# A decoder layer whose weights are split into two fp32r halves: three engines put into program order while Strassen products run

## The chip, the cores and the metric

One core of one Trainium2 chip. The metric is the device time of one execution in microseconds (us). TensorE is called PE here (PEld is its weight load), VectorE DVE, ScalarE ACT, GpSimd POOL and SyncE SP; SP issues the loads.

## The reference

One layer of a hybrid decoder, batch 1, 256 rows, D = 2048, all in fp32:

```
x <- LN0(alpha*x + 0.5*SwiGLU_1(x))                      # FFN 1, 2048 -> 2 x 5504 -> 2048
z  = x @ W_in                                            # nine column groups
m  = sigmoid(gate_conv)*(yA @ Wa) + sigmoid(gate_hgrn)*(yB @ Wb)   # short conv | gated recurrence
x <- LN1(alpha*x + m @ W_out)
x <- LN2(alpha*x + 0.5*SwiGLU_2(x))                      # FFN 2
x <- LN3(alpha*x + sigmoid(x @ W_pg) * (p @ W_pp))
swiglu(x, w_in, w_out): a, u = split(x @ w_in); return (silu(a) * u) @ w_out
```

## The kernel before

**Matrix products.** Every fp32 operand is held as a sum of two fp32r halves, high (h) and low (l), and a product is three matmuls: wh by xh, wl by xh, wh by xl (`passes`, L1052 to L1054). The 256 rows are two row tiles (t = 0, 1) of 128; a pass works on two k blocks of 128 rows of a weight and 512 columns.

**The way of a weight.** SP loads a piece of 256 x 512 into a tile `raw` (`weight_dma`, four of them); ACT casts it to its high half wh (`weight_cast`, L986); DVE subtracts that from raw and gets wl (`weight_split`, L997). There are six pairs of wh and wl (NMAIN) and a few more outside the FFNs (EXTRA). When PE has used a pair up, `consumed` calls `feed`, which issues whatever load, add, cast and split has room.

**An FFN** has 11 chunks of at most 512 columns of a and u. Chunks 0 and 1 are plain products. Chunks 2 to 10 are `Quad`s: one level of Strassen, seven products p1 to p7 in place of eight, with weight sums on DVE (`weight_add`, L965) in tiles of the rings 11, 12, 21, 22. The part of k that doesn't fill a whole step is done by a short step (`ORDER`, 59 passes in a Quad) or by plain passes (`ORDER8`, 60 passes); chunk 2 has the second, chunks 3 to 10 the first. What follows a Quad's products is five steps, `first` to `fifth` in `in_units`: copies on ACT, adds of banks on DVE (`both`, L471), a silu, a product. `turn` then makes the result an operand of the second matrix, three ticks later (a tick is a pass): four transposes on PE into the one bank for transposes (L275), a cast to gh on ACT (L285), a subtraction to gl on DVE (L286). After each of the chunks 2 to 9 come two `out_unit`s, products with w_out of the chunks before; each adds its result to x on DVE (L534).

**Layer norms.** The normalised x is made an operand at once (transposes on PE, `yT` on ACT, L424, xh, xl); g and b are applied to x itself later, in `affine_rows`, one of four column chunks at a time. Before FFN 2 their rows come into one tile, `region["spare"]`, one after the other; `sums`, which makes the Strassen sums of x, waits for that (`settle`).

**What sets the order.** Work is emitted in the program's order with deferred steps (`defer`, by ticks). A tile scheduler then sets each engine's order of instructions by its own timeline; what stands on an engine runs strictly in that order, each instruction waiting for what it needs. FFN 1 runs from 0 to about 700 us of the span, the mixer to 1405, the stage `lead2` and FFN 2 to 2110, then the embedding's product.

Of the kernel before, what the change touches and what calls it, by code (L numbers as in the profile page):

```python
# [10 lines left out]
F32 = mybir.dt.float32  # L11
# [3 lines left out]
ALU = mybir.AluOpType  # L15
PSUM = bass.MemoryType.PSUM

P = 128
D = 2048
S = 256  # L20
NT = 2
DFF = 5504
CW = 1024
CC = 512
# [112 lines left out]
def hybrid_layer(ctx: ExitStack, tc: tile.TileContext, x, p, ln_g, ln_b, ffn1_w_in, ffn1_w_out, mix_w_in,  # L137
                 conv_w, hg_lower_bound, hg_norm_w, branch_w_conv, branch_w_hgrn, mix_w_out,
                 ffn2_w_in, ffn2_w_out, ple_w_gate, ple_w_proj, out):
    nc = tc.nc  # L140
# [7 lines left out]
    op = pool("op", side="left")  # L148
# [4 lines left out]
    region = {}  # L153
# [8 lines left out]
    def open_region(kind):  # L162


        if kind.startswith("tail"):
            region.pop("hctx").close()
        region["pool"] = reopen("ctx", kind, "left")
        region["kind"] = kind
        if kind.startswith("lead"):
            region["high"] = reopen("hctx", kind + "h", "right")  # L170
            held.update(dict.fromkeys(HIGH, 0), on=False)
            region["spare"] = high("11", "spare")
        if kind.startswith("ffn"):
            roles = {"a": 7, "t": 1}
        else:
            roles = {"t": 2, "a": 4, "h": 2}
        free = deque(sorted(banks, key=lambda n: used_at[n]))
        for role, n in roles.items():
            role_of[role] = [free.popleft() for _ in range(n)]
# [5 lines left out]
    ps = pool("ps", space=PSUM)  # L185
# [16 lines left out]
    def defer(delay, fn):  # L202
        insort(later, (state["tick"] + delay, fn), key=lambda e: e[0])
# [37 lines left out]
    def settle(c):  # L241

        while c in unsettled:
            later.pop(0)[1]()
# [63 lines left out]
    def high(part, name):  # L308

        return region["high"].tile([P, KG, CC], F32, tag="b" + part, name=name, bufs=HIGH[part])  # L310
# [5 lines left out]
        return plain[t, c // 2][:, c % 2, :]  # L316

    def sums(stat):
        for c in range(4):
            settle(c)  # L320

        def both(o, a, b, op):
            nc.vector.tensor_tensor(out=o, in0=a, in1=b, op=op)

        def four(x11, x12, x21, x22, s1, s2, s3, s4):
            both(s3, x11, x21, ALU.subtract)
            both(s1, x21, x22, ALU.subtract)
            both(s2, s1, x11, ALU.subtract)
            both(s4, x12, s2, ALU.add)

        lo, hi, spare = [plain[t, 0] for t in range(NT)], [plain[t, 1] for t in range(NT)], region["spare"]
        x = [lo[0][:, 0, :], lo[0][:, 1, :], lo[1][:, 0, :], lo[1][:, 1, :]]
        s3 = spare[:, 0, :]

        def low_sums():
            four(*x, x[2], x[0], s3, x[1])

        def made(n, src):
            halves(stat, n, 0, src, 4, "s")


        short = spare[:, 1, :]

        def short_sums():
            y = [hi[t][:, 0, i * P : (i + 1) * P] for t in range(NT) for i in range(2)]
            four(*y, *(short[:, i * P : (i + 1) * P] for i in range(4)))

        def made_short():
            halves(stat, "short", 0, short, 4, "s")
            h, l = stat.parts["short", 0]  # L350
            for i in range(4):
                stat.parts[f"s{i + 1}", 1] = h[:, i : i + 1, :], l[:, i : i + 1, :]

        def delta(c):
            d = hi[0][:, c % 2, :]
            both(d, d, hi[1][:, c % 2, :], ALU.subtract)
            halves(stat, "d", c, d, 4, "s")

        todo = (low_sums, lambda: made("s1", x[2]), lambda: made("s2", x[0]), lambda: made("s3", s3),
                lambda: made("s4", x[1]), short_sums, made_short, lambda: delta(2), lambda: delta(3),  # L360
                lambda: held.update(on=True))
        for i, fn in enumerate(todo):
            defer(1 + 2 * i, fn)
# [30 lines left out]
        nc.vector.bn_aggr(mv, stats[t])  # L394
        return mv[:, 0:1], rsqrt_of(mv[:, 1:2], 1, 1.0, LN_EPS / scale ** 2)

    def affine_rows(i, c, ts, gb, delay):

        if gb is None:
            gb = rp.tile([P, KG, CC], F32, tag="raw", name="gb", bufs=NRAW)  # L400
        for a, src in enumerate((ln_g, ln_b)):
            nc.sync.dma_start(gb[:, a, :], src[0, i : i + 1, c * CC : (c + 1) * CC].broadcast_to([P, CC]))

        def apply():
            for t in ts:
                xc = xt[t][:, c * CC : (c + 1) * CC]
                nc.vector.tensor_tensor(out=xc, in0=xc, in1=gb[:, 0, :], op=ALU.mult)
                nc.vector.tensor_tensor(out=xc, in0=xc, in1=gb[:, 1, :], op=ALU.add)
            unsettled.remove(c)

        defer(delay, apply)

    def layer_norm(t, i, scale, stat):

        mean, r = moments(t, scale)

        def operand(c, xc):
            y = plain_tile(t, c) if stat is x2 else st.tile([P, CC], F32, tag="silu", name="y", bufs=2)
            tp = transposed(xc, 4)
            if t == 0 and c < 2:  # L420
                gate["pe"] = state["turned"], 1
            for a in range(4):
                k = i * 16 + 4 * c + a
                nc.scalar.activation(y[:, a * P : (a + 1) * P], tp[:, a * P : (a + 1) * P], AF.Identity,  # L424
                                     bias=gbT[:, 48 + k : 49 + k], scale=gbT[:, k : k + 1])
            halves(stat, t, c, y, 4, "x")

        for c in range(4):
            xc = xt[t][:, c * CC : (c + 1) * CC]
            norm = nc.vector.tensor_scalar(out=xc, in0=xc, scalar1=mean, scalar2=r, op0=ALU.subtract, op1=ALU.mult)  # L430
            defer((4 if t else 7 if stat is x2 else 6) + c, lambda c=c, xc=xc: operand(c, xc))
            if c == 1 and t == 0:
                gate["lo"] = norm.ins, 2
        if t == NT - 1:
            for c in range(4):
                unsettled.add(c)
                if stat is x2:
                    defer(2 + 8 * c, lambda c=c: affine_rows(i, c, range(NT), region["spare"], 6))
                else:
                    defer(40 + 20 * c, lambda c=c: affine_rows(i, c, range(NT), None, 4))  # L440

    def layer_norm_out(t, gb):
        mean, r = moments(t, 1.0)
# [9 lines left out]
    def ffn(name, xs, w_in, w_out, ln_i, nxt):  # L453
# [7 lines left out]
        def in_units(ch, g, ci):  # L461
            c0 = starts[ch]
            w = starts[ch + 1] - c0
            if ch > 1:
                made = {}

                def work(tag):
                    return st.tile([P, CC], F32, tag=tag, name=tag, bufs=2 if tag == "silu" else 3)

                def both(o, a, b, op):  # L470
                    nc.vector.tensor_tensor(out=o, in0=a, in1=b, op=op)  # L471

                def first(ps):
                    made["c11"] = work("h")
                    nc.scalar.copy(made["c11"], ps["p1"])

                def second(ps):
                    c = made["c12"] = work("silu")
                    nc.scalar.copy(c, ps["p3"])
                    both(c, c, ps["p5"], ALU.add)  # L480

                def third(ps):
                    e = made["e"] = work("silu")
                    made["c22"] = work("h")
                    both(e, made["c11"], ps["p6"], ALU.add)
                    both(made["c12"], made["c12"], e, ALU.subtract)
                    both(e, e, ps["p7"], ALU.add)
                    both(made["c22"], ps["p5"], e, ALU.subtract)

                def fourth(ps):  # L490
                    h = made["c11"]
                    both(h, h, ps["p2"], ALU.add)
                    nc.scalar.activation(h, h, AF.Silu)
                    both(h, h, made["c12"], ALU.mult)
                    turn(g, 0, ci, h, CC)

                def fifth(ps):
                    e = made["e"]
                    both(e, e, ps["p4"], ALU.add)
                    nc.scalar.activation(e, e, AF.Silu)  # L500
                    both(e, e, made["c22"], ALU.mult)
                    turn(g, 1, ci, e, CC)

                after = deque([(("p1",), first), (("p3", "p5"), second), (("p6", "p7"), third),
                               (("p2",), fourth), (("p4",), fifth)])
                units.append(Quad(xs, w_in, (c0, DFF + c0), CC, after, ch > 2))
                return
            silu = {}

# [564 lines left out]
    def run_quad(u, gi):  # L1074
# [17 lines left out]
            gi += 1  # L1092
        return gi

    gi = 0
    for u in units:
        if isinstance(u, Unit):
            gi = run_unit(u, gi)
        elif isinstance(u, Quad):
            gi = run_quad(u, gi)  # L1100
        else:
            if u[0] == "merge":
                u[1]()
            if region["kind"] != u[0]:
                open_region(u[0])
            if u[0] != "merge":
                u[1]()
            feed()
# [30 lines left out]
```

## Time and profile before

| | |
|---|---|
| median of three runs | 2227.24 us (2227.22 to 2227.46) |
| the profiled execution | 2226.91 us, its span 2225.1 us |
| mean granted PE clock | 0.995 of full speed |
| PE busy | 2192.7 us, 10062 instructions |
| DVE busy | 1753.5 us |
| ACT busy | 1155.2 us |
| DMA | 430 MB, 193 GB/s |

An engine's busy time is how long it worked within the span; the idle time of an engine matters only where another waits for it. In rows of the trace the first number is the start in us, the second how long one instruction or a run of xN takes, then engine, line, operation and tiles (out<-in), and in brackets the idle time just before it and what ended that. The granted clock is the share of full speed that the throttle gave PE.

### The profile page before, as it was taken

The page shows a single profiled execution, that of the slowest core. Times are in us where ns is not written, and L with a number is a line of the kernel's source. Part 1 is how long each engine was busy: PE and PEld are TensorE (multiplying, and loading weights), DVE is VectorE, ACT ScalarE, POOL GpSimd, SP SyncE. Part 2 cuts the span into 40 slices and gives each one's busy share as a digit, 9 for nine tenths or more (in the row PEclk, how much of TensorE's full clock was granted, in tenths as well). Part 3 has the DMA queues.
Part 4 walks back from the last instruction along what each step waited for, and adds up shares of the span by engine and source line. Part 5 has one row for each costly group of instructions (what it writes and reads, how often), then busy time and mean ns, then how long its engine had stood idle before and what let it go on. Part 6 is the DMA issues. An engine that isn't in the chain of part 4 may idle for free.

```text
span 2225.1 us, 27081 instructions
## 1 busy us (share of the span) xinstructions
PE 2192.7 (99%) x10062; PEld 1828.1 (82%) x10062; DVE 1753.5 (79%) x2042; ACT 1155.2 (52%) x1357; POOL 9.8 (0%) x32
## 2 busy tenths in 40 slices
PE   9999999999999999999999999899999999999997
PEld 7987888888887888888888888798788888888886
DVE  6788999999985678567555875669899999999667
ACT  5555565555555434444444443655556555556463
POOL 1000000000000000000000000000000000000000
PEclk9999999999999999999999999999999999999999
DMA  7656666666663665544565655576566666665564
GB/s 252 224 185 198 208 205 190 190 207 208 199 196 118 201 195 171 185 157 151 189 195 183 205 194 192 167 241 188 185 198 204 204 212 194 202 204 188 173 221 152
DMA packets 225848, 430.00 MB, mean 193 GB/s; under 512 B 14252, under 2 KB 22964, under 8 KB 225716
## 3 DMA queue, kind: packets, MB, share of 16 engines
q1 hardware_dynamic: 225716, 428.27, 60.4%
q8 instruction: 79, 1.29, 0.2%
q14 instruction: 53, 0.43, 0.1%
HBM read 426.12 MB, written 2.10 MB: 192 GB/s over the span
## 4 chain that ended last, share of the span: by engine, by line
PE 91%; DVE 5%; DMA 2%; issue 1%; ACT 1%; SPq 0%; DVEq 0%; ACTq 0%
PE bank L1053 29%; PE bank L1054 29%; PE bank L1052 29%; DVE wl L997 2%; PE bank L275 2%; PE bank L644 1%; DVE raw L965 1%; DMA raw<-in_ffn_w_in_dram 1%; DMA spare<-in_ln_g_dram 1%; ACT wh L986 1%; DMA raw<-in_ffn_w_out_dram 0%; DVE x L446 0%; DVE x L447 0%; ACT y L424 0%; DVE x L430 0%
## 5 line engine op out<-in xcount | busy, mean ns | idle before, releaser
L986 ACT CAST wh<-raw 128x1024 fp32r<-128x1024 f32 (+2 forms) x944 | 959.8, 1032 | 833.8 <-PE bank L1054 519.1
L997 DVE TENSOR_TENSOR wl<-raw,wh 128x1024 fp32r<-128x1024 f32 (+2 forms) x944 | 1113.4, 1200 | 286.8 <-ACT wh L986 266.1
L1054 PE MATMUL bank<-wh,xl 128*128 128x512 f32 (+1 forms) x1688 | 652.7, 387 | 5.0 <-DVE xl L286 4.9
L1053 PE MATMUL bank<-wl,xh 128*128 128x512 f32 (+1 forms) x1688 | 652.9, 388 | 0.5 <-DVE wl L997 0.3
L1052 PE MATMUL bank<-wh,xh 128*128 128x512 f32 (+1 forms) x1688 | 648.3, 388 | 1.8 <-ACT xh L285 1.8
L1054 PEld LDWEIGHTS bank<-wh,xl 128*128 128x128 f32 x1688 | 317.9, 188 | 66.5 <-DVE xl L286 6.3
L1052 PEld LDWEIGHTS bank<-wh,xh 128*128 128x128 f32 x1688 | 318.0, 188 | 62.1 <-ACT xh L285 2.5
L1053 PEld LDWEIGHTS bank<-wl,xh 128*128 128x128 f32 x1688 | 318.1, 188 | 61.5 <-DVE wl L997 1.6
L1053 PE MATMUL bank<-wl,gh 128*128 128x512 f32 x896 | 350.6, 392 | 4.5 <-DVE wl L997 4.3
L1054 PE MATMUL bank<-wh,gl 128*128 128x512 f32 x896 | 350.2, 392 | 0.0
L1052 PE MATMUL bank<-wh,gh 128*128 128x512 f32 x896 | 348.9, 393 | 0.0
L965 DVE TENSOR_TENSOR raw<-raw,raw 128x1024 f32<-128x1024 f32 (+1 forms) x176 | 206.3, 1172 | 6.4 <-DMA raw<-in_ffn_w_in_dram 4.7
L1053 PEld LDWEIGHTS bank<-wl,gh 128*128 128x128 f32 x896 | 168.7, 188 | 40.8 <-DVE wl L997 6.4
L1054 PEld LDWEIGHTS bank<-wh,gl 128*128 128x128 f32 x896 | 168.8, 188 | 34.7
L1052 PEld LDWEIGHTS bank<-wh,gh 128*128 128x128 f32 x896 | 168.6, 188 | 34.3 <-ACT gh L285 0.2
L1053 PE MATMUL bank<-wl,sh 128*128 128x512 f32 x464 | 180.8, 390 | 0.0
L1054 PE MATMUL bank<-wh,sl 128*128 128x512 f32 x464 | 180.8, 390 | 0.0
L1052 PE MATMUL bank<-wh,sh 128*128 128x512 f32 x464 | 179.4, 390 | 0.0
L1054 PEld LDWEIGHTS bank<-wh,sl 128*128 128x128 f32 x464 | 87.2, 188 | 18.1
L1053 PEld LDWEIGHTS bank<-wl,sh 128*128 128x128 f32 x464 | 87.2, 188 | 18.0
L1052 PEld LDWEIGHTS bank<-wh,sh 128*128 128x128 f32 x464 | 87.2, 188 | 18.0
L534 DVE TENSOR_TENSOR x<-x,bank 128x512 f32<-128x512 f32 x64 | 43.6, 682 | 21.6 <-PE bank L1054 21.6
(175 smaller groups left out, 1003.6 us busy)
## 6 DMA issues: line engine op xcount, KB each, us to landing
raw<-in_ffn_w_in_dram SPq DMA_DIRECT2D x288, 512.0 KB, 4.4
raw<-in_mix_w_in_dram SPq DMA_DIRECT2D x176, 512.0 KB, 4.7
raw<-in_ffn_w_out_dram SPq DMA_DIRECT2D x168, 512.0 KB, 4.6
raw<-in_ffn_w_in_dram SPq DMA_DIRECT2D x64, 256.0 KB, 3.1
raw<-in_mix_w_out_dram SPq DMA_DIRECT2D x32, 512.0 KB, 5.3
raw<-in_ple_w_gate_dram SPq DMA_DIRECT2D x32, 512.0 KB, 5.1
raw<-in_ffn_w_in_dram SPq DMA_DIRECT2D x32, 384.0 KB, 4.0
raw<-in_branch_w_conv_dram SPq DMA_DIRECT2D x16, 512.0 KB, 5.4
```

Of the source, the lines that this page charges most:

```text
L275: state["turned"] = nc.tensor.transpose(tp[:, i * P : (i + 1) * P], src[:, i * P : (i + 1) * P], ident).ins
L534: nc.vector.tensor_tensor(out=xc, in0=xc, in1=acc, op=ALU.add)
L644: nc.tensor.matmul(gp[:, (h * 2 + t) * 64 : (h * 2 + t + 1) * 64], kd[:, h, t * P : (t + 1) * P], qd[:, h, t, :], start=True, stop=True)
L965: nc.vector.tensor_tensor(out=out, in0=a, in1=b, op=ALU.add)
L986: nc.scalar.copy(h[:, :n, :w], raw[:, :n, :w])
L997: nc.vector.tensor_tensor(out=l[:, :n, :w], in0=raw[:, :n, :w], in1=h[:, :n, :w].bitcast(F32), op=ALU.subtract)
L1052: nc.tensor.matmul(acc, sh, wh[:, a, :n], start=first, stop=False)
L1053: nc.tensor.matmul(acc, sh, wl[:, a, :n], start=False, stop=False)
L1054: nc.tensor.matmul(acc, sl, wh[:, a, :n], start=False, stop=last)
```

## The change

1. From the first Quad of an FFN until the next stage, ACT, DVE and SP run their instructions in program order (`manual_schedule`); the scheduler still sets PE's order.
2. The rows of g and b for the x of FFN 2 are loaded into operand tiles of the tags gh and gl, early (2, 5, 8, 11 ticks after the norm), and applied 12, 14, 16, 18 ticks later. `sums` doesn't wait for them any more, and takes its spare tile from ring 11.
3. Chunk 2 uses the short step too. Three adds and products that follow a Quad are put off by one tick.

```diff
@@ sums
-        for c in range(4):
-            settle(c)
-        lo, hi, spare = [plain[t, 0] for t in range(NT)], [plain[t, 1] for t in range(NT)], region["spare"]
+        lo, hi, spare = [plain[t, 0] for t in range(NT)], [plain[t, 1] for t in range(NT)], high("11", "s")
@@ affine_rows
-        if gb is None:
+        if early:
+            rows = [op.tile([P, CC], F32, tag=tag, name="gb", bufs=8) for tag in ("gh", "gl")]
+        else:
             gb = rp.tile([P, KG, CC], F32, tag="raw", name="gb", bufs=NRAW)
...
-        defer(delay, apply)
+        defer(12 + 2 * c if early else 4, apply)
@@ layer_norm
-                if stat is x2:
-                    defer(2 + 8 * c, lambda c=c: affine_rows(i, c, range(NT), region["spare"], 6))
-                else:
-                    defer(40 + 20 * c, lambda c=c: affine_rows(i, c, range(NT), None, 4))
+                early = stat is x2
+                defer(2 + 3 * c if early else 40 + 20 * c, lambda c=c, early=early: affine_rows(i, c, early))
@@ in_units: second, fourth, fifth
-                    both(c, c, ps["p5"], ALU.add)
+                    defer(1, lambda: both(c, c, ps["p5"], ALU.add))
...
-                    both(h, h, made["c12"], ALU.mult)
+                    defer(1, lambda: both(h, h, made["c12"], ALU.mult))
...
-                    both(e, e, made["c22"], ALU.mult)
+                    defer(1, lambda: both(e, e, made["c22"], ALU.mult))
...
-                units.append(Quad(xs, w_in, (c0, DFF + c0), CC, after, ch > 2))
+                units.append(Quad(xs, w_in, (c0, DFF + c0), CC, after, True))
@@ the loop over units
+    ordered = ExitStack()
+    in_order = {mybir.EngineType.DVE, mybir.EngineType.Activation, mybir.EngineType.SP}
...
         elif isinstance(u, Quad):
+            if "ordered" not in region:
+                region["ordered"] = ordered.enter_context(tc.manual_schedule(engines=in_order))
             gi = run_quad(u, gi)
...
+            if u[0].startswith("tail"):
+                ordered.close()
+                region.pop("ordered")
```

The program has 9891 rows on PE in place of 9897 (six matmuls fewer), 2053 on DVE in place of 2043, 1347 on ACT in place of 1342, 896 on SP in place of 892. Lines of the changed kernel stand 1 to 5 lower (L983 is the cast of L986, L994 the split of L997, L962 the weight sum of L965, L284 and L285 the operand's cast and subtraction, L274 the transposes, L468 the adds of banks, L531 the update of x). Names below carry buffer numbers, which differ between the two kernels.

**FFN 1, the end of chunk 4, ACT.** The product of the chunk is `h` and `silu`; gh are its two operand tiles, wh the weights' high halves. Before:

```order
L986 CAST wh_2301<-raw_2204 128x1024
L986 CAST wh_2313<-raw_2216 128x1024
L986 CAST wh_2325<-raw11_2039 128x1024
L986 CAST wh_2337<-raw_2234 128x1024
L285 CAST gh_2264<-bank1_80 128x512
L500 ACTIVATE silu_2218<-silu_2218 128x512
L986 CAST wh_2378<-raw12_2329 128x1024
L986 CAST wh_2390<-raw21_2146 128x1024
L986 CAST wh_2401<-raw_2249 128x1024
L285 CAST gh_2278<-bank1_80 128x512
L986 CAST wh_2413<-raw21_2146 128x512
```

Three weight casts stood between the two gh casts and four ahead of the first. Now, the same place:

```order
L983 CAST wh_2258<-raw_2199 128x1024
L497 ACTIVATE silu_2231<-silu_2231 128x512
L284 CAST gh_2277<-bank1_80 128x512
L284 CAST gh_2291<-bank1_80 128x512
L983 CAST wh_2314<-raw_2217 128x1024
L983 CAST wh_2326<-raw_2229 128x1024
L983 CAST wh_2338<-raw11_2052 128x1024
L983 CAST wh_2350<-raw_2247 128x1024
```

The two gh casts stand together, and the four weight casts that stood ahead of them stand behind.

**The same place, PE.** `bank1` holds the transposes, and bank6 and bank7 are an out unit's. Before, around the second four transposes (the cast behind gh_2278, wh_2413, is used 42 matmuls further on):

```order
L1052 MATMUL bank7_86<-wh_2313,gh_1790 128x512
L1053 MATMUL bank7_86<-wl_2314,gh_1790 128x512
L1054 MATMUL bank7_86<-wh_2313,gl_1791 128x512
L275 MATMUL bank1_80<-ident_87,silu_2218 128x128 x4
L1052 MATMUL bank3_82<-wh_2325,xh_303 128x512
L1053 MATMUL bank3_82<-wl_2326,xh_303 128x512
L1054 MATMUL bank3_82<-wh_2325,xl_304 128x512
```

The transposes stood behind the out unit, at the next Quad's beginning. Now:

```order
L1050 MATMUL bank7_86<-wl_2259,gh_1315 128x512
L1051 MATMUL bank7_86<-wh_2258,gl_1316 128x512
L274 MATMUL bank1_80<-ident_87,silu_2231 128x128 x4
L1049 MATMUL bank6_85<-wh_2314,gh_1789 128x512
L1049 MATMUL bank7_86<-wh_2314,gh_1803 128x512
L1050 MATMUL bank6_85<-wl_2315,gh_1789 128x512
L1051 MATMUL bank6_85<-wh_2314,gl_1790 128x512
```

They stand inside the out unit, and the matmul right behind them uses wh_2314, the cast right behind the second gh cast on ACT.

**The same place, DVE, now.** gl are the low halves of the chunk's operand tiles:

```order
L468 TENSOR_TENSOR silu_2231<-silu_2231,h_2232 128x512
L285 TENSOR_TENSOR gl_2278<-bank1_80,gh_2277 128x512
L285 TENSOR_TENSOR gl_2292<-bank1_80,gh_2291 128x512
L531 TENSOR_TENSOR x0_94<-x0_94,bank0_79 128x512
L994 TENSOR_TENSOR wl_2315<-raw_2217,wh_2314 128x1024
L994 TENSOR_TENSOR wl_2327<-raw_2229,wh_2326 128x1024
```

The split wl_2315 stands behind both gl and the update of x; the splits of these weights stood ahead of both gl before.

**FFN 1, the end of chunk 2, DVE.** `silu<-h,bank` is an add of `third` that waits for a bank of the Quad. Before:

```order
L997 TENSOR_TENSOR wl_1225<-raw_1087,wh_1224 128x1024
L471 TENSOR_TENSOR silu_1242<-h_1151,bank4_83 128x512
L997 TENSOR_TENSOR wl_1237<-raw_1139,wh_1236 128x512
L997 TENSOR_TENSOR wl_1255<-raw_1195,wh_1254 128x1024
L471 TENSOR_TENSOR silu_1197<-silu_1197,silu_1242 128x512
```

The last weights of the Quad were split behind that add. Now:

```order
L994 TENSOR_TENSOR wl_1220<-raw_1035,wh_1219 128x1024
L994 TENSOR_TENSOR wl_1238<-raw_1100,wh_1237 128x1024
L994 TENSOR_TENSOR wl_1250<-raw_1152,wh_1249 128x512
L468 TENSOR_TENSOR silu_1255<-h_1164,bank7_86 128x512
L468 TENSOR_TENSOR silu_1210<-silu_1210,silu_1255 128x512
```

Three splits stand ahead of it.

**Between mixer and FFN 2, ACT, now.** yT and xh are the operand tiles of the normalised x, the table load and silu belong to chunk 0:

```order
L423 ACTIVATE yT_11207<-bank2_81,gbT_96 128x128 x4
L423 ACTIVATE yT_11207<-bank6_85,gbT_96 128x128 x4
L509 ACT_TABLE_LOAD
L509 ACTIVATE silu_11375<-bank7_86 128x512
L284 CAST xh_11216<-yT_11207 128x512
L423 ACTIVATE yT_11248<-bank2_81,gbT_96 128x128 x4
```

The table load and the silu stood behind all xh casts of both row tiles before.

More of the change, by code (lines that the diff above doesn't have):

```diff
@@ L171, in open_region @@
             held.update(dict.fromkeys(HIGH, 0), on=False)
-            region["spare"] = high("11", "spare")
         if kind.startswith("ffn"):
@@ L395, in moments, with affine_rows @@
         return mv[:, 0:1], rsqrt_of(mv[:, 1:2], 1, 1.0, LN_EPS / scale ** 2)
-    def affine_rows(i, c, ts, gb, delay):
-        if gb is None:
+    def affine_rows(i, c, early):
+        if early:
+            rows = [op.tile([P, CC], F32, tag=tag, name="gb", bufs=8) for tag in ("gh", "gl")]
+        else:
             gb = rp.tile([P, KG, CC], F32, tag="raw", name="gb", bufs=NRAW)
-        for a, src in enumerate((ln_g, ln_b)):
-            nc.sync.dma_start(gb[:, a, :], src[0, i : i + 1, c * CC : (c + 1) * CC].broadcast_to([P, CC]))
+            rows = [gb[:, a, :] for a in range(2)]
+        for w, src in zip(rows, (ln_g, ln_b)):
+            nc.sync.dma_start(w, src[0, i : i + 1, c * CC : (c + 1) * CC].broadcast_to([P, CC]))
         def apply():
-            for t in ts:
+            for t in range(NT):
                 xc = xt[t][:, c * CC : (c + 1) * CC]
-                nc.vector.tensor_tensor(out=xc, in0=xc, in1=gb[:, 0, :], op=ALU.mult)
-                nc.vector.tensor_tensor(out=xc, in0=xc, in1=gb[:, 1, :], op=ALU.add)
+                nc.vector.tensor_tensor(out=xc, in0=xc, in1=rows[0], op=ALU.mult)
+                nc.vector.tensor_tensor(out=xc, in0=xc, in1=rows[1], op=ALU.add)
             unsettled.remove(c)
-        defer(delay, apply)
+        defer(12 + 2 * c if early else 4, apply)
     def layer_norm(t, i, scale, stat):
```

## The prediction

> **What bounds the kernel now.** I read the page first: part 1, part 4, then the steady stretch as windows, and last the places where TensorE stands, engine by engine in time.
>
> ```profile
> PE 2192.7 (99%) x10062; PEld 1828.1 (82%) x10062; DVE 1753.5 (79%) x2042; ACT 1155.2 (52%) x1357; POOL 9.8 (0%) x32
> ...
> PE 91%; DVE 5%; DMA 2%; issue 1%; ACT 1%; SPq 0%; DVEq 0%; ACTq 0%
> ...
> raw<-in_ffn_w_in_dram SPq DMA_DIRECT2D x288, 512.0 KB, 4.4
> ```
>
> PE is busy 99% of 2225.1 us and is 91% of the chain that ended last. So the only ways to a better time are fewer matmuls and shorter PE stalls, and every new PE stall is paid in full. One chunk of each FFN (the same instruction of chunks next to each other) shows it closer; columns are the stretch in us, its length, busy time and count of PE, weight load, DVE, ACT, POOL, then the granted clock, DMA share and GB/s:
>
> ```profile
> 311.65:374.51 62.86, 62.86 (x282) 52.06 (x282) 57.77 (x59) 35.88 (x38) 0.00 (x0) 1.00 0.65 201
> 1718.76:1781.62 62.86, 62.86 (x282) 52.06 (x282) 57.76 (x59) 35.88 (x38) 0.00 (x0) 1.00 0.64 201
> ```
>
> PE has no idle time at all; DVE, with 57.8 of 62.9 us, is the next bound, and ACT and DMA are far off. So the casts and splits keep up now, but DVE can catch up on no more than 5 us per chunk.
>
> Stalls stand elsewhere. At the end of chunk 2, the first Quad of an FFN (rows of DVE, then of PE, in time; in brackets the idle time before the row and what ended it):
>
> ```profile
> 189.58 0.69 DVE L471 TENSOR_TENSOR silu<-h,bank 128x512 f32<-128x512 f32 x1 [2.61 <-PE bank L1054]
> 190.18 1.22 DVE L997 TENSOR_TENSOR wl<-raw,wh 128x1024 fp32r<-128x1024 f32 x1
> ...
> 192.50 0.40 PE L1054 MATMUL bank<-wh,xl 128*128 128x512 f32 x1
> 194.93 0.50 PE L1053 MATMUL bank<-wl,gh 128*128 128x512 f32 x1 [2.02 <-DVE wl L997]
> ...
> 1599.66 0.39 PE L1052 MATMUL bank<-wh,gh 128*128 128x512 f32 x1
> 1600.15 0.50 PE L1053 MATMUL bank<-wl,xh 128*128 128x512 f32 x1
> ...
> 1601.18 0.40 PE L1054 MATMUL bank<-wh,xl 128*128 128x512 f32 x1
> 1603.62 0.50 PE L1053 MATMUL bank<-wl,gh 128*128 128x512 f32 x1 [2.05 <-DVE wl L997]
> ```
>
> DVE waited 2.61 us for a bank with splits queued behind that row, and PE paid: start to start 2.43 us where a matmul takes 0.23. The granted clock after it:
>
> ```profile
> 192.20:195.60 3.40, 1.38 (x6) 0.80 (x6) 3.40 (x4) 0.63 (x1) 0.00 (x0) 1.00 0.54 154
> 195.70:199.00 3.30, 3.30 (x9) 2.56 (x8) 3.30 (x6) 0.36 (x1) 0.00 (x0) 0.50 0.73 236
> 199.10:202.50 3.40, 3.40 (x16) 2.79 (x16) 2.18 (x3) 1.28 (x2) 0.00 (x0) 1.00 0.91 301
> 1601.90:1605.30 3.40, 1.68 (x7) 1.40 (x8) 3.40 (x5) 0.06 (x1) 0.00 (x0) 1.00 0.48 167
> 1605.40:1608.80 3.40, 3.40 (x17) 2.80 (x16) 3.40 (x6) 1.05 (x1) 0.00 (x0) 1.00 0.91 308
> ```
>
> After 3.4 us with PE busy 1.38 (idle 2.02) the clock was 0.50 for the next 3.4 us; after 3.4 us with 1.68 busy (idle 1.72) it stayed 1.00. A slow stretch fits 8 or 9 matmuls where a full one fits 15 (3.41 / 0.227): it costs 7 x 0.227 = 1.6 us.
>
> **The change, part by part.**
>
> *Matmuls.* Chunk 2 with the short step has 59 passes instead of 60; a pass fewer is three matmuls, twice: 6 x 0.227 = -1.4 us. The pitch is from this pair, 27 starts apart, (402.72 - 396.58) / 27 = 0.2274:
>
> ```profile
> 396.58 0.40 PE L1052 MATMUL bank<-wh,gh 128*128 128x512 f32 x1
> ...
> 402.72 0.39 PE L1052 MATMUL bank<-wh,gh 128*128 128x512 f32 x1
> ```
>
> *The end of chunk 2.* In the new order of DVE three splits stand ahead of the add that waits for the bank, so PE's next weights are ready when that wait comes. Lost there now: 2.43 - 0.23 = 2.2 in each FFN, 1.6 for the slow stretch in the first, and some 0.95 in each for three or four starts that come 0.1 to 0.3 us late (1599.66 to 1600.15 is one, 0.49 where 0.23 would do): 4.4 + 1.6 + 1.9 = 7.9. I take all of it as gone: -7.9 (bounds 0 and -7.9).
>
> *The ends of chunks 2 to 9: a new wait.* This is the costly part. In the new program order of ACT both gh casts of a chunk's product stand next to each other and the next weight cast behind them; the second gh cast waits for the second four transposes, and the matmul that stands right behind those transposes on PE needs that weight cast. On DVE both gl and an x update stand ahead of its split. Before, 42 matmuls (9.6 us) lay between the transposes and the first use of the cast behind the second gh. The order shows the pattern 8 times in each FFN, 16 in all. Durations for the chain, all from one place of the steady stretch:
>
> ```profile
> 394.75 0.60 PE L275 MATMUL bank<-ident,h 128*128 128x128 f32 x4
> 395.11 0.48 PE L1052 MATMUL bank<-wh,gh 128*128 128x512 f32 x1
> 395.42 0.40 PE L1053 MATMUL bank<-wl,gh 128*128 128x512 f32 x1
> 395.66 0.40 PE L1054 MATMUL bank<-wh,gl 128*128 128x512 f32 x1
> ...
> 395.39 0.59 ACT L285 CAST gh<-bank 128x512 fp32r<-128x512 f32 x1 [0.71 <-PE bank L275]
> 395.87 0.64 ACT L500 ACTIVATE silu<-silu 128x512 f32<-128x512 f32 x1
> ...
> 403.82 0.59 ACT L285 CAST gh<-bank 128x512 fp32r<-128x512 f32 x1 [2.52 <-PE bank L275]
> ...
> 406.86 1.05 ACT L986 CAST wh<-raw 128x1024 fp32r<-128x1024 f32 x1 [0.75 <-PE bank L1054]
> ...
> 395.52 0.68 DVE L534 TENSOR_TENSOR x<-x,bank 128x512 f32<-128x512 f32 x1
> 396.11 1.22 DVE L997 TENSOR_TENSOR wl<-raw,wh 128x1024 fp32r<-128x1024 f32 x1
> 397.25 0.69 DVE L286 TENSOR_TENSOR gl<-bank,gh 128x512 fp32r<-128x512 f32 x1
> 397.85 0.68 DVE L471 TENSOR_TENSOR silu<-silu,h 128x512 f32<-128x512 f32 x1
> ...
> 404.44 0.69 DVE L286 TENSOR_TENSOR gl<-bank,gh 128x512 fp32r<-128x512 f32 x1 [0.56 <-ACT gh L285]
> ```
>
> Counting from the end of the transposes (395.35): gh starts at +0.04, the next ACT instruction 0.48 later (395.39 to 395.87), and the weight cast takes 1.05: PE can go on at about +1.6. DVE: gl starts 0.62 after gh (403.82 to 404.44), its pitch is 0.60 (397.25 to 397.85), the x update's 0.59 (395.52 to 396.11), the split takes 1.22: +0.04 +0.62 +0.60 +0.59 +1.22 = 3.07, and PE's first matmul with that split at about +3.1. Unstalled it starts as the third behind the transposes, at +0.31 (395.66). So a place costs 3.1 - 0.3 = 2.8 us. The lower bound is 2.3 (without the x update), the upper 3.4 (DVE one 0.6 us row late); each step is forced by the order of one engine, so I see no cover. 16 x 2.8 = +45.
>
> *The clock at these places.* The stall leaves PE idle for 2.6 us in two pieces (0 to 1.55 and 2.05 to 3.1). A 3.41 us window catches 2.02 of it, which halved the clock above, in 43% of phases, and 1.72, which did not, in 60%: 7 to 10 of the 16 places. I take 8 x 1.6 = +13; bounds 0 and 16 x 1.6 = 26.
>
> The Trainium skill, "TensorE: Matmul & The Clock Gate", section "What's actually happening", gives the slow clock to the default state and to one at least wholly idle window of some 3.4 us. No place here would empty a window, so by it the +13 is 0 and the sum 2265. The trace disagrees: the window at 192.20 was busy 1.38 us and the next ran at 0.50.
>
> *Rows of g and b in operand tiles.* Between the mixer and the second FFN:
>
> ```profile
> 1415.07 0.69 DVE L407 TENSOR_TENSOR x<-x,spare 128x512 f32<-128x512 f32 x1 [2.84 <-DMA spare<-in_ln_g_dram]
> ...
> 1417.67 0.80 PE L1054 MATMUL bank<-wh,xl 128*128 128x512 f32 x1 [4.20 <-DVE xl L286]
> ...
> 1439.09 1.28 ACT L512 ACT_TABLE_LOAD   x1
> 1440.38 0.60 ACT L512 ACTIVATE silu<-bank 128x512 f32<-128x512 f32 x1
> ```
>
> DVE waits 2.84 us for a row of g, and PE stands 4.20 us for xl behind it. With the rows loaded early that wait goes; but the xh cast ahead of this xl stands behind a weight cast that waits for its own load, and six multiplies of 0.60 (3.6 us) come into DVE's queue: I cost this at 0. The table load and silu (1.28 + 0.60), last on ACT now, stand in the new order ahead of xh casts of the second row tile: +2, what they take. Bounds -5 (4.20 and a slow stretch gone in part) and +5. Take +2.
>
> *The rest.* DVE gets ten rows more, ACT five, SP four. At 1.2 us DVE's are 12 us, hidden under PE with 2225 - 1754 = 471 us idle; without that cover 12. The load queue SP now issues strictly in program order, a load behind one whose slot is late: with 4.4 us to landing and DMA at 0.65 I cost it at 0; a load that is late adds up to 4.4. The multiplies put off by a tick move nothing on PE: 0, or 0.6 each on a chunk where DVE is late.
>
> **Sum**, on the profiled execution's span: 2225.1 - 1.4 - 7.9 + 45 + 13 + 2 = 2275.8. That execution took 2226.91 us, 1.8 beyond its span, and the median of the three runs is 0.3 above it: 2278.
>
> **Rivals.**
>
> 1. The clock stays at 1.00 at the 16 places: 2278 - 13 = 2265. For it, 1603.62 (idle 1.72 in its window, no slow stretch); against it, 195.70.
> 2. It halves at nearly all: 2278 + 13 = 2291. The stalls recur at one spacing, so the phases need not be spread.
> 3. DVE becomes the bound inside the Quads: in program order each of its waits for a bank holds back the splits, as the 2.61 us did. At 0.5 us in each of 18 Quads +9, 2287; at the 2.02 us of 194.93 +36, 2314. Against it: 5 us of slack per chunk, and the added stalls give DVE time.
> 4. The other side, not slower: the queued casts at the 16 places are covered after all, because ACT and DVE reach them while PE still has matmuls whose weights are split. It decides at (7.9 + 1.4) / 16 = 0.58 us a place: below that the kernel is faster; with nothing lost, 2227.2 - 9.3 = 2218. For it speaks only that DVE and ACT kept pace in the steady chunk; against it, that the weight cast stands behind the gh cast and that behind the transposes, with no matmul between them and the one that needs it.
> 5. The change does not do what it says: excluded, the new rows stand in program order.
>
> **How the numbers follow.** Chances: main case (7 to 10 slow windows, 2270 to 2286) 0.50; rival 1, 0.18; rival 2, 0.11; rival 3, 0.14; rival 4, 0.06; something else 0.01. The predicted time is the main case's, 2278. The range: from below 16 x 2.3 and no slow stretch, 2227.2 - 9.3 + 37 - 2 = 2253; from above 16 x 3.4 with 16 slow stretches, 2227.2 - 9.3 + 54 + 26 + 2 = 2300. What this measurement can tell from no change is about 0.2%, 4.5 us. Only rival 4 and a remainder end below 2231.7: slower 0.94, faster 0.05, same 0.01.
>
> **What would show it.** In the changed kernel's waits, PE should wait 16 times for the weight cast and 16 times for its split, each pair behind four transposes, 2.8 us together; the chunk period should go from 62.9 to 65.7 or 67.3; the granted clock should fall to 0.50 behind about half of these places; the 2 us waits at 194.93 and 1603.62 should be gone; PE's busy share should drop to some 97%. I am wrong if PE has matmuls left while the second gh cast runs, if the split is there at +1.6, or if DVE's waits for banks grow.

## The result and the profile after: 3.6% slower, more than the range allowed

The changed kernel took 2309.38 us in the median of four runs (2306.75 to 2310.1), the kernel before 2227.35 beside it: a ratio of 1.0363 with a 95% interval of 1.035 to 1.0376. The direction was right, the size was not: +82 us in place of +51, and 9 us above the range's upper end. The profiled execution took 2309.94 us with a span of 2308.2, 83.1 more than before.

From the page of the changed kernel, the busy time of the engines and the chain that ended last:

```profile
PE 2228.3 (97%) x10056; PEld 1838.1 (80%) x10056; DVE 1768.8 (77%) x2052; ACT 1141.8 (49%) x1362; POOL 10.1 (0%) x32
...
PE 81%; DVE 9%; ACT 5%; issue 3%; DMA 2%; ACTq 0%; DVEq 0%; SPq 0%
```

PE is 81% of the chain in place of 91%, ACT and DVE have 14% in place of 6%. PE's busy time rose by 36 us with six matmuls fewer, so none of it is work: 13 more windows of 3.41 us at the slow clock (20 in place of 7), at 1.6 us each, are 21 of them; the other 15 were not assigned. What PE waited for, in us in total, times, and the longest:

```profile
PE bank L1049 <- ACT wh L983: 33.1, 31, 1.6
PE bank L1050 <- DVE wl L994: 16.6, 18, 2.8
```

The kernel before has no such line for the cast. Two chunks, from one second set of transposes to the next, in the columns used for the windows before:

```profile
414.15:481.62 67.47, 65.08 (x283) 53.09 (x282) 58.09 (x58) 34.52 (x38) 0.00 (x0) 0.97 0.58 187
481.62:548.38 66.76, 63.96 (x282) 51.84 (x281) 58.00 (x58) 34.52 (x38) 0.00 (x0) 1.00 0.59 189
```

A chunk takes 67.5 us with a slow stretch in it and 66.8 without, where it took 62.9. One of the 16 places in time, PE, ACT, DVE:

```profile
481.62 0.60 PE L274 MATMUL bank<-ident,silu 128*128 128x128 f32 x4
483.83 0.73 PE L1049 MATMUL bank<-wh,gh 128*128 128x512 f32 x2 [1.62 <-ACT wh L983]
485.34 0.50 PE L1050 MATMUL bank<-wl,gh 128*128 128x512 f32 x1 [0.78 <-DVE wl L994]
...
482.25 0.58 ACT L284 CAST gh<-bank 128x512 fp32r<-128x512 f32 x1 [2.63 <-PE bank L274]
482.73 3.89 ACT L983 CAST wh<-raw 128x1024 fp32r<-128x1024 f32 x4
...
482.87 0.69 DVE L285 TENSOR_TENSOR gl<-bank,gh 128x512 fp32r<-128x512 f32 x1 [2.52 <-ACT gh L284]
483.48 0.68 DVE L531 TENSOR_TENSOR x<-x,bank 128x512 f32<-128x512 f32 x1
484.07 3.49 DVE L994 TENSOR_TENSOR wl<-raw,wh 128x1024 fp32r<-128x1024 f32 x3
```

The chain is the forecast one: transposes end at 482.22, PE goes on 1.61 us later with wh and 3.12 us later with wl. All 16 places look so; each costs 2.9 us in late starts. A second kind of stall, which the prediction's sum does not have, stands inside Quads:

```profile
526.85 1.22 DVE L962 TENSOR_TENSOR raw<-raw,raw 128x1024 f32<-128x1024 f32 x1
529.26 2.36 DVE L994 TENSOR_TENSOR wl<-raw,wh 128x1024 fp32r<-128x1024 f32 x2 [1.19 <-ACT wh L983]
...
528.18 2.00 ACT L983 CAST wh<-raw 128x1024 fp32r<-128x1024 f32 x2 [2.50 <-DVE raw L962]
...
530.23 0.50 PE L1049 MATMUL bank<-wh,gh 128*128 128x512 f32 x1 [0.40 <-ACT wh L983]
```

DVE makes a weight sum, ACT waits for it and casts it, and DVE waits 1.19 us for the cast: the split is next in its order, and nothing behind it can pass. PE catches up with the casts and waits 0.40 us. At the end of FFN 1, behind another such sum, PE waited 2.65 us for a split:

```profile
670.46 0.50 PE L1050 MATMUL bank<-wl,gh 128*128 128x512 f32 x1 [2.65 <-DVE wl L994]
```

Adding up PE's late starts (start to start beyond 0.227 us for a matmul) in both traces gives where the 83 us are (the stalls of the kernel before that the prediction puts at the end of chunk 2 are at the end of chunk 3, see below):

| | us |
|---|---|
| the 16 places, 2.93 each | +46.9 |
| slow clock behind 10 of them, 1.6 each | +16 |
| 11 stalls of 0.66 to 0.78 inside Quads | +8.1 |
| ends of FFN 1 and FFN 2, slow stretches included | +13.4 |
| between mixer and FFN 2 (13.9 in place of 9.8) | +4.1 |
| start of the mixer (5.1 in place of 3.0) | +2.1 |
| end of chunk 3, both FFNs | -7.8 |
| six matmuls | -1.4 |
| not assigned | +1.7 |

### The profile page after: what moved, and what is told of

Its sections match the earlier page's. It is cut to its first block, busy times and chain, and to the rows that moved or that the text cites. A ratio compares the mean times of both kernels' runs of the same rounds, so it can differ in the third digit from the quotient of the medians.

```text
span 2308.2 us, 27063 instructions
## 1 busy us (share of the span) xinstructions
PE 2228.3 (97%) x10056; PEld 1838.1 (80%) x10056; DVE 1768.8 (77%) x2052; ACT 1141.8 (49%) x1362; POOL 10.1 (0%) x32
## 4 chain that ended last, share of the span: by engine, by line
PE 81%; DVE 9%; ACT 5%; issue 3%; DMA 2%; ACTq 0%; DVEq 0%; SPq 0%
PE bank L1050 26%; PE bank L1051 26%; PE bank L1049 26%; DVE wl L994 4%; ACT wh L983 3%; DVE raw L962 3%; PE bank L274 1%; DMA raw<-in_ffn_w_out_dram 1%; PE bank L641 1%; ACT gh L284 0%; ACT y L423 0%; DVE x L443 0%; DVE x L531 0%; DVE x L444 0%; DMA raw<-in_ffn_w_in_dram 0%
## 5 line engine op out<-in xcount | busy, mean ns | idle before, releaser
L983 ACT CAST wh<-raw 128x1024 fp32r<-128x1024 f32 (+2 forms) x948 | 948.1, 1030 | 868.9 <-PE bank L1051 385.2
L994 DVE TENSOR_TENSOR wl<-raw,wh 128x1024 fp32r<-128x1024 f32 (+2 forms) x948 | 1117.4, 1197 | 281.2 <-ACT wh L983 261.8
L1049 PE MATMUL bank<-wh,xh 128*128 128x512 f32 (+1 forms) x1682 | 639.4, 389 | 6.2 <-ACT xh L284 3.0
L1050 PE MATMUL bank<-wl,gh 128*128 128x512 f32 x896 | 358.9, 401 | 14.8 <-DVE wl L994 14.8
L1050 PEld LDWEIGHTS bank<-wl,xh 128*128 128x128 f32 x1682 | 317.3, 189 | 63.2 <-DVE wl L994 2.1
L1051 PE MATMUL bank<-wh,gl 128*128 128x512 f32 x896 | 357.0, 399 | 0.0
L962 DVE TENSOR_TENSOR raw<-raw,raw 128x1024 f32<-128x1024 f32 (+1 forms) x180 | 209.9, 1166 | 2.8 <-DMA raw<-in_ffn_w_in_dram 1.6
L1049 PE MATMUL bank<-wh,sh 128*128 128x512 f32 x468 | 172.8, 392 | 0.1
L285 DVE TENSOR_TENSOR gl<-bank,gh 128x512 fp32r<-128x512 f32 (+2 forms) x50 | 33.2, 666 | 64.3 <-ACT gh L284 64.3
```

The source lines that it names most:

```text
L285: nc.vector.tensor_tensor(out=lf, in0=src, in1=hf.bitcast(F32), op=ALU.subtract)
L962: nc.vector.tensor_tensor(out=out, in0=a, in1=b, op=ALU.add)
L983: nc.scalar.copy(h[:, :n, :w], raw[:, :n, :w])
L994: nc.vector.tensor_tensor(out=l[:, :n, :w], in0=raw[:, :n, :w], in1=h[:, :n, :w].bitcast(F32), op=ALU.subtract)
L1049: nc.tensor.matmul(acc, sh, wh[:, a, :n], start=first, stop=False)
L1050: nc.tensor.matmul(acc, sh, wl[:, a, :n], start=False, stop=False)
```

## The experiments

Theory A was that the casts queued behind the gh casts make the loss; theory B, that DVE's program order does; theory C, that the other parts have a share. Two more came after the first four runs: theory D, that in program order DVE is the bound, and theory E, that what is left are fixed waits of PE at a few instructions.

**Without the program order.**

```diff
-            if "ordered" not in region:
-                region["ordered"] = ordered.enter_context(tc.manual_schedule(engines=in_order))
...
-            if u[0].startswith("tail"):
-                ordered.close()
-                region.pop("ordered")
```

> The changed kernel without the program order: ACT, DVE and SP are set by the scheduler as before; the rows of g and b in operand tiles and the short step in chunk 2 stay. Theory A (the loss is the program order): 2218 to 2230 us, no wait for a weight cast behind transposes. Theory C (the other two parts carry a share of the loss, by the rows' loads or the new step): 2240 us or more.

2232.93 us, ratio 1.0023 (1.0011 to 1.0035): between the two forecasts, 3 us above A's and 7 below C's. So the program order carries nearly all of the loss. The rest of the change costs 5 us by itself. Without the order the stalls at the ends of the first Quads are not gone, and there are three in place of two: chunk 2, with the short step now, stalls in both FFNs (4.2 us around 134, 4.3 at 1543), chunk 3 in FFN 2 alone (4.3 at 1608). DVE at the end of chunk 2 in this run:

```profile
128.73 0.69 DVE L468 TENSOR_TENSOR silu<-h,bank 128x512 f32<-128x512 f32 x1 [2.77 <-PE bank L1051]
```

**The program order and nothing else.**

```diff
+    ordered = ExitStack()
+    in_order = {mybir.EngineType.DVE, mybir.EngineType.Activation, mybir.EngineType.SP}
...
         elif isinstance(u, Quad):
+            if "ordered" not in region:
+                region["ordered"] = ordered.enter_context(tc.manual_schedule(engines=in_order))
             gi = run_quad(u, gi)
...
+            if u[0].startswith("tail"):
+                ordered.close()
+                region.pop("ordered")
```

> The kernel before with the program order on ACT, DVE and SP and nothing else of the change (chunk 2 as before, rows of g and b through the spare tile). If the order is the loss and the other two parts matter little under it: 2300 to 2320 us. If the other two parts save time once the order is fixed (the 7.9 us at chunk 2): above 2315 us, and the wait at the end of chunk 2 stays.

2305.55 us, 1.035 (1.032 to 1.0381). The waits at the end of chunk 3 are gone here too, and nothing else of the change is in this run: so the -7.8 us come from the order. The short step of chunk 2 has no part in them.

**One engine at a time.**

```diff
-    in_order = {mybir.EngineType.DVE, mybir.EngineType.Activation, mybir.EngineType.SP}
+    in_order = {mybir.EngineType.Activation}      # the first run;   {mybir.EngineType.DVE} in the second
```

> Program order on ACT alone, DVE by the scheduler. In the order 0 matmuls lie between the second transposes and the first use of the cast behind the second gh cast, 16 times, as in the changed kernel. Theory A (the cast queued behind the gh cast makes the loss): the 16 waits for the cast stay, each 1.3 us or more, with some slow clock: 2255 to 2300 us. Theory B (DVE in program order makes it, its waits for banks and sums hold back the splits): 2235 us or less.

> Program order on DVE alone, ACT by the scheduler. In the order 21 to 27 matmuls (4.8 to 6.1 us) lie between the second transposes and the first use of the cast behind the second gh. Theory A: the 16 waits are gone, since 3.1 us of chain fit into 4.8: 2218 to 2240 us. Theory B: most of the loss stays: 2280 us or more.

ACT alone: 2315.55 us, 1.0393 (1.0363 to 1.0423). DVE alone: 2329.22 us, 1.0454 (1.0424 to 1.0485). B's forecast for DVE alone came in, the other three did not, and neither theory stands as written: each engine's order by itself costs more than both together. PE's waits, of the run with ACT, then of the run with DVE:

```profile
PE bank L1050 <- DVE wl L994: 37.1, 46, 3.3
PE bank L1049 <- ACT wh L983: 25.9, 16, 1.6
```

```profile
PE bank L1050 <- DVE wl L994: 57.4, 21, 3.3
```

With DVE alone the waits for the cast are gone, as A said of ACT, but the splits stand behind the second gl all the same. One such place:

```profile
488.96 0.60 PE L274 MATMUL bank<-ident,silu 128*128 128x128 f32 x4
492.69 0.54 PE L1050 MATMUL bank<-wl,gh 128*128 128x512 f32 x1 [3.13 <-DVE wl L994]
...
490.22 0.69 DVE L285 TENSOR_TENSOR gl<-bank,gh 128x512 fp32r<-128x512 f32 x1 [1.84 <-ACT gh L284]
490.82 0.68 DVE L531 TENSOR_TENSOR x<-x,bank 128x512 f32<-128x512 f32 x1
491.42 3.49 DVE L994 TENSOR_TENSOR wl<-raw,wh 128x1024 fp32r<-128x1024 f32 x3
```

The mechanism is one on two engines: weight work queued behind work on an operand that waits for PE itself. With DVE alone PE idles in one piece of 3.13 us, and the slow clock came at 15 of the 16 places (10 in the changed kernel). With ACT alone the 16 places stay, and 14 times a Quad's splits come late behind an add that waits for a bank, 2.1 us each in late starts (DVE, then PE):

```profile
464.04 0.69 DVE L468 TENSOR_TENSOR silu<-h,bank 128x512 f32<-128x512 f32 x1 [3.28 <-PE bank L1051]
...
465.92 0.50 PE L1050 MATMUL bank<-wl,xh 128*128 128x512 f32 x1 [0.33 <-DVE wl L994]
468.78 0.51 PE L1050 MATMUL bank<-wl,gh 128*128 128x512 f32 x1 [1.21 <-DVE wl L994]
```

This is the stall of chunk 3 in the kernel before. With DVE in program order, alone or with the others, that add waits for its bank in none of the 18 Quads.

**The turn three ticks later.** In program order some casts and splits then come ahead of gh and gl.

```diff
-            defer(3, lambda: to_stat(g, t, ci, h, w // P, "g"))
+            defer(6, lambda: to_stat(g, t, ci, h, w // P, "g"))
```

> The changed kernel with one number changed: the product is turned 6 ticks after its last step in place of 3, so that casts come ahead of the gh casts in program order; in the order 10 or 12 matmuls (2.3 or 2.7 us) lie now between the second transposes and the use of the cast behind the second gh. Theory A: a chain of 3.1 us less 2.3 to 2.7 leaves 0 to 0.6 us a place and no slow clock there: 16 x 2.9 + 10 x 1.6 = 63 us go, 2246 us (2240 to 2256). Theory B: DVE's order is as strict as before, 2290 us or more.

2276.81 us, 1.0219 (1.019 to 1.0249): 33 us gone, not 63. The 16 stalls and their slow clock are gone, as A said, but the chunk still takes 65.4 us (before: 62.9): PE waits in small pieces, and DVE waits in line. A chunk, and DVE's waits over 5.7 chunks (270 to 640 us):

```profile
406.40:471.80 65.40, 64.30 (x282) 51.57 (x281) 58.16 (x59) 34.54 (x38) 0.00 (x0) 1.00 0.60 193
```

```profile
DVE wl L994 <- ACT wh L983: 18.7, 34, 1.2
DVE gl L285 <- ACT gh L284: 11.5, 12, 1.0
DVE silu L468 <- ACT silu L497: 4.2, 6, 0.7
DVE h L468 <- ACT h L490: 3.5, 5, 0.7
```

37.9 us of waits in 5.7 chunks are 6.7 a chunk; with 58.2 of work that is 64.9 of the 65.4 us. In the kernel before all of DVE's waits in the same 370 us are 24.9 us in 5.9 chunks, 4.2 a chunk, 62.0 with its work, and the wait for gh is a fifth of what it is here:

```profile
DVE wl L997 <- ACT wh L986: 18.7, 29, 2.2
DVE gl L286 <- ACT gh L285: 2.2, 4, 0.6
```

Hence theory D: in program order DVE is the bound; the big stall had hidden it, since PE's standing gave DVE time.

**A split between a sum and its cast.** In the Quad's order of elements, t4 is a sum made from the ring of 21, and stood right behind it; a plain pass now stands between (with the turn after 6 ticks):

```diff
-    ORDER = ("h1 u0 h2 h3 a0 h4 11.0 u1 t1.0 22.0 t3.0 a1 t2.0 21.0 t4.0 "
-             "11.1 u2 t1.1 22.1 t3.1 a2 t2.1 21.1 t4.1").split()
+    ORDER = ("h1 u0 h2 h3 a0 h4 11.0 u1 t1.0 22.0 t3.0 t2.0 21.0 a1 t4.0 "
+             "11.1 u2 t1.1 22.1 t3.1 t2.1 21.1 a2 t4.1").split()
```

> The kernel with the product turned after 6 ticks, and in the Quad's order of elements one plain pass each moved between 21 and t4, so that DVE has a split to do while ACT casts the sum t4. Theory D (DVE is the bound in program order: its 58.2 us a chunk and some 6.7 us in which it waits for casts make the 65.4 us period of that kernel): about 1.2 us go twice a Quad, up to 18 x 2.4 = 43, 2234 to 2262 us. Theory E (the rest of the loss is fixed waits of PE at a few instructions, DVE has slack): no change, 2272 to 2280 us.

2249.51 us, 1.0099 (1.007 to 1.0128): 27 us gone by the order of elements alone, as D said; the stall at the end of FFN 1 went with it (1.6 us in place of 7.6), the one at the end of FFN 2 did not (5.2 with its slow clock). That one is now a load: ACT's cast waits for it, and PE for the cast. Why the load is late was not tried.

```profile
2065.77 1.04 ACT L983 CAST wh<-raw 128x1024 fp32r<-128x1024 f32 x1 [2.49 <-DMA raw<-in_ffn_w_out_dram]
2068.86 1.65 PE L1049 MATMUL bank<-wh,gh 128*128 128x512 f32 x3 [2.92 <-ACT wh L983]
```

Through the middle of a Quad DVE has hardly a pause now (49.45 of 50 us), and the chunk is 1.1 us above 62.9:

```profile
464.66:528.70 64.04, 63.90 (x283) 51.76 (x282) 58.07 (x59) 34.65 (x38) 0.00 (x0) 1.00 0.62 197
467.00:517.00 50.00, 49.86 (x217) 40.17 (x216) 49.45 (x48) 28.50 (x31) 0.00 (x0) 1.00 0.64 210
```

**Two sums of each Quad left out**, in that kernel.

```diff
-        nc.vector.tensor_tensor(out=out, in0=a, in1=b, op=ALU.add)
+        if short or el["use"][0][0] != "p4":
+            nc.vector.tensor_tensor(out=out, in0=a, in1=b, op=ALU.add)
```

> The kernel with 6 ticks and the changed order of elements, leaving out the two sums t4 of each Quad (1.2 us each on DVE, the cast then takes raw as it is; nothing changes on PE). Theory D (DVE runs without a pause through the 50 us of a Quad and holds PE back by the 1.1 us by which the chunk is still above 62.9): the chunk falls to 62.9 and 17 to 22 us go, 2228 to 2236 us. If the 1.1 us are fixed waits of PE: 2244 us or more.

2233.0 us, 1.0027 (1.0016 to 1.0037): 16.5 us less: the time is inside D's forecast, the gain just under its 17 to 22 us, and the chunk fell to 63.2 and not all the way to 62.9:

```profile
462.10:525.30 63.20, 63.14 (x283) 51.86 (x282) 55.64 (x56) 34.43 (x38) 0.00 (x0) 1.00 0.62 200
```

**The additions to x left out**, in the kernel with 6 ticks.

```diff
@@ epi_o
-                else:
+                elif last:
                     nc.vector.tensor_tensor(out=xc, in0=xc, in1=acc, op=ALU.add)
```

> The kernel with the product turned after 6 ticks, leaving out the additions of the out units to x after chunks 4 to 9 (four of 0.60 us a chunk on DVE, nothing on PE). Theory D: DVE's period falls by up to 2.4 us in 12 chunks, 29 us: 2248 to 2262 us. Theory E: 2274 to 2278 us.

2263.43 us, 1.0161 (1.0129 to 1.0193): 13 us gone, about half of what these instructions take, between the two theories and 1.4 us above D's range. They stand at the out units, where DVE also waits for gh and silu, and the other half went into DVE's own waits: in the same 370 us these grew from 37.9 to 44.5 us, 1.1 us a chunk. So D holds inside the Quads; over the whole chunk, less work on DVE gives back only what its waits leave of it.

**DVE's other waits spread.** Relative to the kernel with the new order of elements:

```diff
-        nc.vector.tensor_tensor(out=lf, in0=src, in1=hf.bitcast(F32), op=ALU.subtract)
-        stat.parts[t, g] = (h, l)
+        def low():
+            nc.vector.tensor_tensor(out=lf, in0=src, in1=hf.bitcast(F32), op=ALU.subtract)
+            stat.parts[t, g] = (h, l)
+        if tag == "g" and "ordered" in region:
+            defer(1, low)
+        else:
+            low()
...
-            defer(6, lambda: to_stat(g, t, ci, h, w // P, "g"))
+            defer((7, 10)[t], lambda: to_stat(g, t, ci, h, w // P, "g"))
...
-                    defer(1, lambda: both(h, h, made["c12"], ALU.mult))
+                    defer(2, lambda: both(h, h, made["c12"], ALU.mult))
...
-                    defer(1, lambda: both(e, e, made["c22"], ALU.mult))
+                    defer(2, lambda: both(e, e, made["c22"], ALU.mult))
```

> As the run before, and DVE's other waits in line are spread: the products behind a silu 2 ticks later in place of 1, the subtraction to gl one tick behind its cast, and the two row tiles turned after 7 and 10 ticks. Theory D: DVE's waits fall under the 5 us that a chunk of 62.9 us leaves it, 2225 to 2245 us, about the kernel before. Theory E: 2265 us or more.

2257.22 us, 1.0133 (1.0104 to 1.0163): a miss, 8 us more than without these edits. The waits for gh and silu are gone from DVE's list, and one larger took their place (200 to 640 us):

```profile
DVE wl L1001 <- ACT wh L990: 43.7, 21, 4.7
```

Splits stand in line for their casts, 2.1 us in the mean and up to 4.7, where these waits were 8.4 us in the run before: what was spread in one place was queued in another. Why these casts come late was not tried.

**The order of elements without program order.** The same edit to `ORDER` in the run without program order, and in the kernel before, there also:

```diff
     ORDER8 = ("u3 a3 11.0 u0 t1.0 a0 22.0 t3.0 u1 t2.0 21.0 a1 t4.0 "
-              "11.1 u2 t1.1 22.1 t3.1 a2 t2.1 21.1 t4.1").split()
+              "11.1 u2 t1.1 22.1 t3.1 t2.1 21.1 a2 t4.1").split()
```

> All engines by the scheduler, the changed rows of g and b, the short step in every chunk, and the Quad's order with a pass between 21 and t4. If the order of elements helps wherever DVE is near its bound: 2218 to 2230 us, and the 13 us lost around chunk 2 in the run without program order shrink. If it helps only where DVE can't run ahead: as that run, 2231 to 2236 us.

> The kernel before with one edit: the Quad's order with a pass between 21 and t4. The chunk of the kernel before has no idle time on PE, so theory D gives 0 for chunks 3 to 10; at the end of chunk 2 the 7.9 us may go or not: 2219 to 2229 us.

2220.11 us, 0.9967 (0.9955 to 0.998), and 2221.4 us, 0.9971 (0.9962 to 0.998): both beat the kernel before by 0.3%, and the changed kernel by 4%. The 13 us of stalls at chunks 2 and 3 are gone from the first, the 7.8 at chunk 3 from the second. A chunk stays at PE's bound, as D said; here of the first:

```profile
460.20:523.00 62.80, 62.80 (x282) 52.01 (x281) 57.58 (x58) 35.41 (x39) 0.00 (x0) 1.00 0.62 201
```

## Why the prediction was wrong in size

- *The new wait at the ends of chunks 2 to 9*: right. 2.8 us were forecast, 2.93 measured, 16 times; its parts (1.57 and 3.07 us behind the transposes in the working, 1.61 and 3.12 in the trace) to 0.05 us.
- *The clock*: 8 slow stretches at these places were taken, 10 came, +16 in place of +13.
- *The end of chunk 2*: -7.9 forecast, -7.8 measured, but the place was misread, and the agreement is in part luck. The wait at 189.58 and its twin in FFN 2, at 1598.27, belong to the second Quad, chunk 3; the same add of chunk 2, whose order was shown, waited for nothing at 130.66. It came right because the program order does there what it does at chunk 2: three splits now stand ahead of the add. Before, at chunk 2; now, at chunk 3:

```profile
130.66 0.68 DVE L471 TENSOR_TENSOR silu<-h,bank 128x512 f32<-128x512 f32 x1
...
198.41 2.96 DVE L994 TENSOR_TENSOR wl<-raw,wh 128x1024 fp32r<-128x1024 f32 x3
201.29 0.68 DVE L468 TENSOR_TENSOR silu<-h,bank 128x512 f32<-128x512 f32 x1
```

- *Matmuls*: -1.4, as counted.
- *Rows of g and b, between mixer and FFN 2*: +2 forecast, +4.1 measured, inside the bounds. The forecast wait is there: PE stood 1.76 us for the xh cast behind the table load and the silu. A slow stretch of 1.6 us behind it was not in the term. The wait for xl fell only from 4.20 to 3.40 us.

```profile
1474.44 1.28 ACT L509 ACT_TABLE_LOAD   x1
...
1476.89 0.79 PE L1049 MATMUL bank<-wh,xh 128*128 128x512 f32 x1 [1.76 <-ACT xh L284]
```

- *The rest, costed at nothing*: the step that failed. DVE's rows were called hidden under 471 us of idle time, an average over the whole kernel; in a Quad DVE has far less, and in program order it also waits in line. This is rival 3, with a chance of 0.14, and the 8.1 us inside the Quads are 0.45 us a Quad, next to its price of 0.5. Its mechanism was another: DVE's waits in line are for ACT's casts, not for banks. It came together with the main case, not in its place: 8.1 us inside the Quads and 13.4 at the ends of the FFNs. Rival 3's argument against itself, that the stalls give DVE time, held: with the 16 stalls gone the chunk came only to 65.4 us. But the range took the rivals one at a time and added none to the main case: 2278 and the 30.7 us by which the terms of this list were off make 2309. Its upper end also took two terms at -7.9 and +2 whose own bounds were 0 and +5; with these it would be 2311, and would have covered the time by luck, since those are not the terms that were off by much. A late load, costed at 0 or up to 4.4 us, shows once: the 2.9 us at the end of FFN 2 with the new order of elements.
- *The start of the mixer*: +2.1, not looked for. It is there in the runs that have DVE in program order, the rest of the change and the old order of elements, and not in the run with the order alone or in any with the new order of elements; its cause was not tried.
- *Rivals 1, 2 and 4*: 10 of 16 slow stretches is the upper end of the main case's 7 to 10, so neither 1 nor 2 came; no place was covered, so 4 fell.

Shown by runs: that the program order makes the loss, that it does so on ACT and on DVE each, that under it the turn's place makes the 16 stalls, and that DVE in line holds back the Quads. Open are the late load at the end of FFN 2 and the start of the mixer. Why either engine alone is worse than both was seen only in part: with DVE alone the one-piece stall and its slow clock; with ACT alone the 14 delays by splits. Of the 23 us that the kernel with the new order and 6 ticks keeps, the sums left out gave back 16.5; the rest wasn't tried.

## What to carry to other kernels

An engine that runs in the order in which the work is written waits in that order: whatever stands behind work that depends on the bottleneck itself is late by the whole round trip, so put the bottleneck's next inputs ahead of it. Count the slack of the next engine in the stretch where it is busiest, with its waits in line, and not as the average over the span; and where one stall hides another bound, add the second to the range. Between a producer and its consumer that go through another engine, a piece of other work in line is worth much of the wait: here one pass moved in each half of a Quad gave 27 us, of at most 43, in program order, and 13 or 6 without it.

## What the runs showed of the hardware

The clock's rule is sharper than the two windows before could tell. The slow stretches lie on a grid of 3.413 us. Over thirteen traces of this study (without the first and the last 20 us, windows that ran at full clock, PE's busy time as the profile gives it): all 71 windows with PE busy up to 1.64 us were followed by 0.50, none of 248 with 1.86 to 3.1 us was, and of 25 between them 7 were. So about half a window of busy time decides. Two pairs in the changed kernel, of the same stall of 2.9 us at two phases:

```profile
415.30:418.70 3.40, 1.55 (x6) 0.98 (x7) 3.30 (x4) 3.40 (x5) 0.00 (x0) 1.00 0.01 2
418.70:422.10 3.40, 3.40 (x10) 2.66 (x9) 3.40 (x4) 1.24 (x2) 0.00 (x0) 0.50 0.87 270
278.80:282.20 3.40, 1.78 (x10) 1.25 (x8) 0.96 (x2) 1.58 (x3) 0.00 (x0) 1.00 0.00 0
282.20:285.60 3.40, 2.62 (x10) 1.88 (x11) 3.40 (x4) 2.79 (x3) 0.00 (x0) 1.00 0.21 32
```

With 1.55 us busy the next window is slow, with 1.78 it is not, and no window here is empty: the rule of an idle window in the Trainium skill, "TensorE: Matmul & The Clock Gate", section "What's actually happening", does not hold for this case.
